# Batches of small matrix products in a recurrent scan: each batch queued behind one leader, and a 32-column product widened to 128

## The chip, the cores and the metric

The kernel runs on one core of a Trainium2 chip. The metric is the device time of one launch in microseconds (us); of the kernel before there are three timed runs with a median of 1272.58 us.

## The reference, cut to what matters

The model is a trunk of two residual layers over 512 tokens of width 1024. Layer 0 mixes tokens with a gated spatial MLP, layer 1 with an RWKV-7 recurrence; each is followed by a gated convolutional FFN, and a last RMSNorm ends it. The change lies in the recurrence, which has 16 heads of width 64:

```python
def step(state, inp):
    r_t, w_t, k_t, v_t, a_t, b_t = inp
    sa = jnp.einsum('bhvk,bhk->bhv', state, a_t)
    state = (state * w_t[:, :, None, :]
             + sa[..., None] * b_t[:, :, None, :]
             + v_t[..., None] * k_t[:, :, None, :])
    y_t = jnp.einsum('bhvk,bhk->bhv', state, r_t)
    return state, y_t
...
g = jax.nn.sigmoid(xg @ g1) @ g2          # g1: 1024 x 160, g2: 160 x 1024
...
return (y * g) @ w_o
```

The kernel doesn't step token by token. It cuts the 512 tokens into 8 chunks of 64 and does each chunk with small matrix products, so that only the 64 x 64 state of each head goes from chunk to chunk. The gate `g` needs a product with the 160 columns of `g1`, which the kernel does as 128 columns and 32 columns.

## The kernel before, in words

**The big products.** Nearly all arithmetic is 512 columns wide on TensorE. Each fp32 factor is split into a high and a low part, and a product becomes three matmuls, `mm3` (L313, its matmuls are L317, L318 and L319). Weights stream in from HBM ahead of their use.

**The scan.** `scan(g)` (L1168) runs for two groups g of 8 heads, one after the other, and in each over 8 chunks c. The 8 heads of a group are 4 pairs i of 2 heads `hd`; head `hd` = 0 lies on partitions 0 to 63, `hd` = 1 on 64 to 127. One chunk has five batches of 8 small products on TensorE, one for each `(i, hd)` in the list `ih`, and between them copies that hand the result on:

- L1194 (128 rows in, 64 columns out) makes `us` from the operand `vu`, which holds the state and the values of the chunk. L1196 copies `us` to `wt` on VectorE.
- L1198, of the same shape, makes the part of the output `e` that needs the same `vu` only.
- L1207 (64 x 64) multiplies `wt` by an inverse computed earlier. L1208 copies half 0 of the result into `vu` on VectorE, and L1209 copies half 1 on ScalarE.
- L1216 (128 x 64) makes the next state from `vu`. L1219 adds the decayed old state, half 0 and then half 1, on VectorE, and that is the operand `vu` of the next chunk's L1194.
- L1221 (64 x 64) adds the rest of `e`, which L1224 copies out on ScalarE.

So a chunk is a chain: L1194, L1196, L1207, L1208 and L1209, L1216, L1219, and again L1194. In two of these handovers the half `hd` = 1 is written after the half `hd` = 0.

**The filler.** While the chain waits for VectorE or ScalarE, TensorE does other work that is due anyway. `weave` advances the generator `fill`, which holds the value projections, the gates (`gates`, L1061) and the output projection (`project`), and queues each piece behind a mark in the chain; `side` is the inversion of the other group (L1030 and L1033, 32 x 32 products). `finish` (transposes, L1247) and `value` (L829, L844) come in between too. A scheduler then puts all instructions of an engine in one fixed order; with `tc.issue_after(x)` an instruction is kept behind x in the order of its engine, without a wait. In the scan before, the small products have no such order among them, and the scheduler may place each one by itself.

**The gate product.** `gates` multiplies 512 tokens by the 160 columns of `g1` in 8 steps over k. Each step has `mm3` with 128 columns and then `mm3` with 32 columns (128 rows in, 32 columns out); the 32 columns of each k lie next to each other in one weight tile, 256 columns in all. `gate_parts` (L300) loads it.

Of the kernel before, what the change touches and what calls it, by code (L numbers as in the profile page):

```python
# [12 lines left out]
F32 = mybir.dt.float32  # L13
F32R = mybir.dt.float32r
# [6 lines left out]
P = 128  # L21
D = 1024
KT = 8
# [121 lines left out]
class Emit:  # L145
# [154 lines left out]
    def gate_parts(self):  # L300

        t = [self.wp.tile([P, 1024], F32, tag="w32", bufs=2, name=self.uid("w32")) for _ in range(2)]
        for i in range(2):
            self.wq.dma_start(t[i], self.gd[:, i, 0:1024])
        return (1024, [tuple(x.bitcast(F32R) for x in t)]), (512, [self.pair(self.gd[:, :, 1024:], 256)])

    @staticmethod
    def wcols(w, c, n, rows=slice(None)):
# [423 lines left out]
    def rwkv_main(self, r, ctx, gain):  # L732
# [328 lines left out]
        def gates():  # L1061


            ws = ga["parts"]
            accs = [self.acc("mm")[0:n] for n in (P, 32)]
            for k in range(KT):
                x = gx[k]
                if k + 2 < KT:
                    gx.append(gate_mix(k + 2))
                for a, w, n in zip(accs, ws, (P, 32)):  # L1070
                    self.mm3(a, self.wcols(w, k * n, n), x, k == 0, k == KT - 1)
                next(tail[0], None)
                if k >= 3:
                    back(k - 3)
                yield
            for k in range(KT - 3, KT):
                back(k)
            for i, a in enumerate(accs):
                t = scratch("sq")[0:(P, 32)[i]]
                S.activation(t, a, AF.Tanh, scale=0.5)  # L1080
                V.tensor_scalar(t, t, 0.5, 0.5, ALU.mult, ALU.add)
                if i == 0:
                    S.copy(r.sg[0], t)
                    V.tensor_tensor(r.sg[1], t, r.sg[0].bitcast(F32), ALU.subtract)
                else:
                    self.stack(r.sg[2], t)
                yield
# [79 lines left out]

        def scan(g, late=iter(())):  # L1168

            ih = [(i, hd) for i in range(4) for hd in range(2)]  # L1170
            y = None

            for c in range(NCH):
                last = c == NCH - 1
# [10 lines left out]
                def ar(i, hd, n):  # L1185
                    o = C + P * hd + n * C
                    return st[i][:, o:o + C]

                def pt(i, hd):
                    o = RW * (1 - hd)  # L1190
                    return st[i][H[hd], o:o + C]

                for i, hd in ih:
                    nc.tensor.matmul(us[H[hd], 0, i, :], ar(i, hd, 0), vu[:, hd, i, :], start=True, stop=True)  # L1194
                wt = tile_([P, 4, C], "wt", 4)
                V.tensor_copy(wt, us[:, 0])  # L1196
                for i, hd in ih:
                    nc.tensor.matmul(e[H[hd], 0, i, :], ar(i, hd, 1), vu[:, hd, i, :],  # L1198
                                     start=i == 0, stop=False, skip_group_check=True)
                if not last:  # L1200
                    s0 = tile_([P, 4, C], "wt", 4)
                    for hd in range(2):
# [8 lines left out]
                if g == 1 and c == 0:  # L1211
                    self.step(late)
                yield
                if not last:
                    for i, hd in ih:
                        nc.tensor.matmul(us[H[hd], 0, i, :], bt[:, i, hd, :], vu[:, hd, i, :], start=True, stop=True)  # L1216
                    nvu = chunks[g, c + 1][2]
                    for hd in range(2):
                        V.tensor_tensor(nvu[H[hd], hd], us[H[hd], 0], s0[H[hd]], ALU.add)  # L1219
                for i, hd in ih:  # L1220
                    nc.tensor.matmul(e[H[hd], 0, i, :], pt(i, hd), vu[H[hd], hd, i, :],  # L1221
                                     start=False, stop=True, skip_group_check=True)
                for hd in range(2):
                    S.copy(y[H[c % 2], :, hd, :], e[H[hd], 0])  # L1224
                self.step(late)
# [169 lines left out]
```

## Time and profile before

| what | value |
|---|---|
| timed runs | 1272.14, 1272.58 and 1272.93 us; median 1272.58 us |
| the profiled execution's own time | 1274.33 us |
| its span, from the first to the last instruction | 1272.5 us |
| TensorE matmuls busy | 1254.8 us (99%) |
| TensorE weight loads busy | 1014.3 us (80%) |
| VectorE busy | 856.5 us (67%) |
| ScalarE busy | 629.6 us (49%) |
| GpSimd busy | 98.0 us (8%) |
| mean granted clock of TensorE | 0.994 |
| the stretch from 737 to 862 us, which holds the two scans: TensorE busy | 120.61 of 125.00 us |

In a timeline row the first number is the start in us, the second the length of the row, then the engine (PE is TensorE, DVE VectorE, ACT ScalarE, POOL GpSimd, PEld TensorE's weight loads), the line, the operation, out<-in by names, the size of the stationary operand (rows*columns), the shape, and how many records the row merges. The ends of matmuls are modelled and overlap the next matmul; what TensorE spends on something is read from one start to the next. A small fp32 product leaves two records, a batch of 8 leaves 16; a big one (`mm3`) leaves one record per matmul. Brackets at the end give the idle time ahead of a row and what ended it.

### The profile page before, as it was taken

The numbers are of one execution on the slowest core, as the hardware profiler recorded it, in microseconds if no ns is written. First come the engines' busy times: TensorE is split into PE (matmuls) and PEld (weight loads), VectorE is DVE, ScalarE is ACT, GpSimd is POOL, SyncE is SP. The second block draws the span as 40 slices with busy tenths as digits, with TensorE's granted clock in tenths as the row PEclk, the third lists the DMA queues.
The fourth block names the chain that finished last, engine by engine and source line by source line (L and its number), as shares of the span: only waits on it lengthen the run. The fifth ranks groups of instructions, "written<-read, shape, count | busy, mean of one in ns | idle before, by whom it ended". The sixth has DMA issues, their size and how long they took to land.

```text
span 1272.5 us, 19534 instructions
## 1 busy us (share of the span) xinstructions
PE 1254.8 (99%) x7591; PEld 1014.3 (80%) x7591; DVE 856.5 (67%) x1403; ACT 629.6 (49%) x1082; POOL 98.0 (8%) x119
## 2 busy tenths in 40 slices
PE   9999999999999999999999999999999999999997
PEld 6878888888888888887777776677888888888886
DVE  6466568888886444675789887665677777772233
ACT  5534446555555333475686647423544444443232
POOL 4100200000000000000000022222100000000002
PEclk9999999999999999999999999999999999999999
DMA  7332357887556775335878698763233332233332
GB/s 251 108 99 83 123 173 239 244 255 240 198 169 209 216 231 161 105 106 182 220 203 226 202 245 206 203 181 133 83 99 100 100 99 91 94 94 106 93 91 79
DMA packets 115452, 201.65 MB, mean 158 GB/s; under 512 B 21600, under 2 KB 53600, under 8 KB 115360
## 3 DMA queue, kind: packets, MB, share of 16 engines
q10 hardware_dynamic: 39104, 112.87, 29.4%
q1 hardware_dynamic: 76256, 87.54, 23.1%
q8 instruction: 59, 0.97, 0.3%
q14 instruction: 33, 0.27, 0.1%
HBM read 152.93 MB, written 47.45 MB: 157 GB/s over the span
## 4 chain that ended last, share of the span: by engine, by line
PE 90%; DVE 4%; issue 1%; DMA 0%; POOL 0%; ACT 0%; DVEq 0%; ACTq 0%; POOLq 0%
PE mm L317 10%; PE mm L319 9%; PE mm L318 9%; PE aux L317 6%; PE aux L319 6%; PE aux L318 6%; PE e L318 6%; PE e L317 6%; PE e L319 6%; PE us L319 5%; PE us L318 5%; PE us L317 5%; PE aux L935 1%; PE aux L949 1%; PE us L1194 1%; PE e L1221 1%
## 5 line engine op out<-in xcount | busy, mean ns | idle before, releaser
L236 ACT CAST w<-w 128x512 fp32r<-128x512 f32 x340 | 206.8, 611 | 364.6 <-PE aux L319 91.8
L237 DVE TENSOR_TENSOR w<-w,w 128x512 fp32r<-128x512 f32 x340 | 232.1, 685 | 185.2 <-ACT w L236 184.7
L317 PE MATMUL mm<-mxh,w 128*128 128x512 f32 (+1 forms) x416 | 170.5, 410 | 0.0
L318 PE MATMUL mm<-mxl,w 128*128 128x512 f32 (+1 forms) x416 | 164.6, 396 | 0.0
L319 PE MATMUL mm<-mxh,w 128*128 128x512 f32 (+1 forms) x416 | 164.3, 395 | 0.0
L344 POOL TENSOR_TENSOR ss<-ss,sq 128x512 f32<-128x512 f32 x30 | 40.6, 1353 | 771.1 <-issue 592.9
L317 PEld LDWEIGHTS mm<-mxh,w 128*128 128x128 f32 (+1 forms) x416 | 77.6, 187 | 20.0 <-issue 3.3
L319 PEld LDWEIGHTS mm<-mxh,w 128*128 128x128 f32 (+1 forms) x416 | 77.8, 187 | 17.4 <-issue 0.7
L318 PEld LDWEIGHTS mm<-mxl,w 128*128 128x128 f32 (+1 forms) x416 | 77.9, 187 | 16.1 <-issue 1.3
L542 ACT ACTIVATE cv<-z,par 128x512 f32<-128x512 f32 x88 | 71.7, 817 | 28.1 <-DVE z L540 23.1
L317 PE MATMUL aux<-mxh,w 128*128 128x512 f32 x216 | 84.5, 391 | 0.0
L319 PE MATMUL aux<-mxh,w 128*128 128x512 f32 x216 | 84.2, 390 | 0.3 <-DVE w L237 0.3
L317 PE MATMUL us<-mxh,w 128*128 128x512 f32 x216 | 84.5, 391 | 0.0
L318 PE MATMUL aux<-mxl,w 128*128 128x512 f32 x216 | 84.1, 389 | 0.0
L318 PE MATMUL us<-mxl,w 128*128 128x512 f32 x216 | 84.1, 389 | 0.0
L319 PE MATMUL us<-mxh,w 128*128 128x512 f32 x216 | 84.0, 389 | 0.0
L317 PE MATMUL e<-mxh,w 128*128 128x512 f32 x208 | 81.4, 391 | 0.1
L318 PE MATMUL e<-mxl,w 128*128 128x512 f32 x208 | 81.1, 390 | 0.1
L319 PE MATMUL e<-mxh,w 128*128 128x512 f32 x208 | 80.9, 389 | 0.0
L543 DVE SCALAR_TENSOR_TENSOR cv<-z,par,cv 128x512 f32<-128x512 f32 x88 | 66.1, 752 | 20.0 <-ACT cv L542 20.0
L544 DVE SCALAR_TENSOR_TENSOR cv<-z,par,cv 128x512 f32<-128x512 f32 x88 | 66.0, 752 | 2.9
L319 PEld LDWEIGHTS aux<-mxh,w 128*128 128x128 f32 x216 | 40.5, 187 | 9.2 <-DVE w L237 0.8
(1088 smaller groups left out, 2599.0 us busy)
## 6 DMA issues: line engine op xcount, KB each, us to landing
w<-in_wup ACTq DMA_DIRECT2D x88, 512.0 KB, 3.7
w<-in_wdn ACTq DMA_DIRECT2D x32, 512.0 KB, 3.6
st<-std SPq DMA_DIRECT2D x30, 320.0 KB, 6.1
w<-wkd ACTq DMA_DIRECT2D x16, 512.0 KB, 4.8
w<-wvd ACTq DMA_DIRECT2D x16, 512.0 KB, 5.6
w<-wod ACTq DMA_DIRECT2D x16, 512.0 KB, 4.3
w<-in_wdn ACTq DMA_DIRECT2D x16, 384.0 KB, 3.3
w<-in_wsu ACTq DMA_DIRECT2D x8, 512.0 KB, 3.8
```

The source lines that it names most:

```text
L236: nc.scalar.copy(hi[r, :n], src)
L237: (lo_eng or nc.vector).tensor_tensor(lo[r, :n], src, hi[r, :n].bitcast(F32), ALU.subtract)
L317: mm(acc, wh, xh, start=first, stop=False)
L318: mm(acc, wh, xl, start=False, stop=False)
L319: mm(acc, wl, xh, start=False, stop=last)
L344: nc.gpsimd.tensor_tensor(self.ss, self.ss, self.sq, ALU.add)
L542: nc.scalar.activation(c, z[:, 2:], AF.Identity, scale=cw(2, i), bias=self.p("conv_b", l * 44 + i))
L543: nc.vector.scalar_tensor_tensor(c, z[:, 1:T + 1], cw(1, i), c, ALU.mult, ALU.add)
L544: nc.vector.scalar_tensor_tensor(c, z[:, 0:T], cw(0, i), c, ALU.mult, ALU.add)
L935: nc.tensor.matmul(qs[hd][:, c - ch.start, :], bk[H[hd], c, C * hd:C * hd + P], ar[H[hd], c, :], start=True, stop=True)
L949: nc.tensor.matmul(qs[hd][:, c, :], bk[H[hd], c, C * hd:C * hd + P], dg[H[hd], c, :], start=True, stop=True)
L1194: nc.tensor.matmul(us[H[hd], 0, i, :], ar(i, hd, 0), vu[:, hd, i, :], start=True, stop=True)
```

## The change

Two things are changed. In `scan` a helper `batch` emits the 8 products of a batch; the list `ih` now has `hd` = 1 ahead of `hd` = 0 in each pair, and all products of a batch after the first are kept behind the first in TensorE's order (the leader). L1198's batch is kept behind the leader of L1194, and L1221's batch behind the leader of L1216. The batch of L1207 has the new order of `ih`, but no leader. In the gates the 32-column product now takes 128 columns: its own 32 and the 96 behind them in the tile; the accumulator has 128 rows, of which the last 96 are not read. The tile's columns 256 to 383, which no load fills, are set to zero on GpSimd.

```diff
@@ gate_parts
-        return (1024, [...]), (512, [self.pair(self.gd[:, :, 1024:], 256)])
+        w = self.pair(self.gd[:, :, 1024:], 256)
+        for x in w:
+            self.nc.gpsimd.memset(x[:, 256:384].bitcast(F32), 0.0)
+        return (1024, [...]), (512, [w])
@@ gates
-            accs = [self.acc("mm")[0:n] for n in (P, 32)]
+            accs = [self.acc("mm") for _ in range(2)]
...
-                    self.mm3(a, self.wcols(w, k * n, n), x, k == 0, k == KT - 1)
+                    self.mm3(a, self.wcols(w, k * n, P), x, k == 0, k == KT - 1)
...
-                S.activation(t, a, AF.Tanh, scale=0.5)
+                S.activation(t, a[0:(P, 32)[i]], AF.Tanh, scale=0.5)
@@ scan
-            ih = [(i, hd) for i in range(4) for hd in range(2)]
+            ih = [(i, hd) for i in range(4) for hd in (1, 0)]
+            def batch(one, lead=None):
+                for n, (i, hd) in enumerate(ih):
+                    with ExitStack() as behind:
+                        if lead is not None:
+                            behind.enter_context(tc.issue_after(lead))
+                        one(i, hd, n)
+                    if lead is None:
+                        lead = self.last(mybir.EngineType.PE)
+                return lead
...
-                for i, hd in ih:
-                    nc.tensor.matmul(us[H[hd], 0, i, :], ar(i, hd, 0), vu[:, hd, i, :], start=True, stop=True)
+                lead = batch(lambda i, hd, n: nc.tensor.matmul(us[H[hd], 0, i, :], ar(i, hd, 0), vu[:, hd, i, :],
+                                                               start=True, stop=True))
...
-                for i, hd in ih:
-                    nc.tensor.matmul(e[H[hd], 0, i, :], ar(i, hd, 1), ...)
+                batch(lambda i, hd, n: nc.tensor.matmul(e[H[hd], 0, i, :], ar(i, hd, 1), ...), lead)
...
+                lead = None
                 if not last:
-                    for i, hd in ih:
-                        nc.tensor.matmul(us[H[hd], 0, i, :], bt[:, i, hd, :], vu[:, hd, i, :], start=True, stop=True)
+                    lead = batch(lambda i, hd, n: nc.tensor.matmul(us[H[hd], 0, i, :], bt[:, i, hd, :], ...))
...
-                for i, hd in ih:
-                    nc.tensor.matmul(e[H[hd], 0, i, :], pt(i, hd), vu[H[hd], hd, i, :], ...)
+                batch(lambda i, hd, n: nc.tensor.matmul(e[H[hd], 0, i, :], pt(i, hd), ...), lead)
```

The order of the changed kernel prints its own line numbers. There L1207 and L1211 are the batches L1194 and L1198 of before, L1220 is L1207, L1229 is L1216, L1234 is L1221, L320 to L322 are L317 to L319, L832 is L829, L1107 is L1104 and L1260 is L1247.

TensorE's order in the first scan, from the end of a chunk into the next (in the trace of before this is 756.68 to 761.97 us). `us` and `e` are the accumulators of the batches, `mm` those of the filler. Before:

```order
L1221 MATMUL e_6839<-vu_6742,st_6738 64x64
L829 MATMUL mm_6982<-cst,v_6903 128x128 x3
L1216 MATMUL us_6838<-vu_6742,cbt_6741 64x64 x8
L1221 MATMUL e_6839<-vu_6742,st_6738 64x64 x7
L829 MATMUL mm_6982<-cst,v_6903 128x128
L317 MATMUL mm_6905<-mxh_5515,w_1094_6701 128x512
L1194 MATMUL us_6945<-vu_6742,st_6834 64x64
L1198 MATMUL e_6946<-vu_6742,st_6834 64x64
L318 MATMUL mm_6905<-mxl_5516,w_1094_6701 128x512
L1194 MATMUL us_6945<-vu_6742,st_6834 64x64 x7
L1198 MATMUL e_6946<-vu_6742,st_6834 64x64 x7
L1247 MATMUL aux_6968<-cst,y_6656 128x128 x4
```

The same place in the changed kernel:

```order
L832 MATMUL mm_6982<-cst,v_6903 128x128 x3
L1229 MATMUL us_6838<-vu_6742,cbt_6741 64x64 x8
L1234 MATMUL e_6839<-vu_6742,st_6738 64x64 x8
L832 MATMUL mm_6982<-cst,v_6903 128x128
L320 MATMUL mm_6905<-mxh_5515,w_1094_6701 128x512
L321 MATMUL mm_6905<-mxl_5516,w_1094_6701 128x512
L322 MATMUL mm_6905<-mxh_5515,w_1094_6701 128x512
L1207 MATMUL us_6945<-vu_6742,st_6834 64x64 x8
L1211 MATMUL e_6946<-vu_6742,st_6834 64x64 x8
L1260 MATMUL aux_6968<-cst,y_6656 128x128 x4
```

The single product that stood ahead of the filler is back in its batch, the pair ahead of L318 is back in its batches, and the filler that stood between the pair and the rest now stands ahead of both.

TensorE's order in the second scan, where the filler is the gate of one head group (accumulators `aux`; 814.93 to 820.06 us in the trace of before). Before:

```order
L1104 MATMUL aux_7775<-sg_6635,gw_6992 128x512
L317 MATMUL aux_7814<-sg_6633,gwh_6996 128x512
L318 MATMUL aux_7814<-sg_6634,gwh_6996 128x512
L1221 MATMUL e_7710<-vu_7533,st_7611 64x64
L319 MATMUL aux_7814<-sg_6633,gwl_6997 128x512
L1104 MATMUL aux_7814<-sg_6635,gw_6992 128x512
L1216 MATMUL us_7709<-vu_7533,cbt_7532 64x64 x8
L1221 MATMUL e_7710<-vu_7533,st_7611 64x64 x7
L1194 MATMUL us_7789<-vu_7705,st_7701 64x64
L1198 MATMUL e_7790<-vu_7705,st_7701 64x64
L1194 MATMUL us_7789<-vu_7705,st_7701 64x64 x7
L1198 MATMUL e_7790<-vu_7705,st_7701 64x64 x7
```

The same place in the changed kernel:

```order
L320 MATMUL aux_7816<-sg_6633,gwh_6996 128x512
L321 MATMUL aux_7816<-sg_6634,gwh_6996 128x512
L322 MATMUL aux_7816<-sg_6633,gwl_6997 128x512
L1229 MATMUL us_7711<-vu_7535,cbt_7534 64x64 x8
L1234 MATMUL e_7712<-vu_7535,st_7613 64x64 x8
L1107 MATMUL aux_7777<-sg_6635,gw_6992 128x512
L1107 MATMUL aux_7816<-sg_6635,gw_6992 128x512
L1207 MATMUL us_7791<-vu_7707,st_7703 64x64 x8
L1211 MATMUL e_7792<-vu_7707,st_7703 64x64 x8
```

Here the single product is back in its batch too, the pair had no filler behind it before, and the two products of L1104 moved from ahead of L1216 to between L1221 and the next chunk. Outside the two scans TensorE's order is the same in both kernels, SP's is the same everywhere, and VectorE and ScalarE have the same instructions with some of the filler's moved by a place or a few.

12 lines of the change are left out of this document (7 added, 5 removed).

## The prediction

> **What bounds the kernel now.** I read the page first, then busy time by stretches, then TensorE's timeline in the scan. The head of the page:
>
> ```profile
> span 1272.5 us, 19534 instructions
> PE 1254.8 (99%) x7591; PEld 1014.3 (80%) x7591; DVE 856.5 (67%) x1403; ACT 629.6 (49%) x1082; POOL 98.0 (8%) x119
> ```
>
> TensorE is busy for all but 18 us, so a gain has to be TensorE time. The stretch that holds both scans, and all behind it (columns: length, then busy time and records of PE, PEld, DVE, ACT, POOL, then granted clock, DMA share, GB/s):
>
> ```profile
> 737.00:862.00 125.00, 120.61 (x1754) 87.64 (x1753) 91.99 (x203) 59.63 (x120) 31.12 (x35) 1.00 0.80 205
> 865.00:1272.50 407.50, 397.57 (x1843) 331.70 (x1841) 245.51 (x369) 169.77 (x273) 23.86 (x24) 0.99 0.31 97
> ```
>
> The scan has few real waits, 4.4 us of 125. Behind it TensorE's order is unchanged and TensorE is nearly full, so what the scan saves stays saved at the end. But busy isn't useful here. TensorE's timeline around a single product of L1221 that stands alone in the filler, and a whole batch further on:
>
> ```profile
> 755.66 0.40 PE L319 MATMUL mm<-mxh,w 128*128 128x512 f32 x1
> 755.89 0.39 PE L317 MATMUL mm<-mxh,w 128*128 128x512 f32 x1
> ...
> 756.35 0.40 PE L319 MATMUL mm<-mxh,w 128*128 128x512 f32 x1
> 756.68 0.32 PE L1221 MATMUL e<-vu,st 64*64 64x64 f32 x2
> 756.94 0.94 PE L829 MATMUL mm<-cst,v 128*128 128x128 f32 x6
> ...
> 763.08 0.68 PE L1207 MATMUL us<-wt,ti 64*64 64x64 f32 x16
> 763.69 0.50 PE L317 MATMUL mm<-mxh,w 128*128 128x512 f32 x1
> 764.03 0.39 PE L318 MATMUL mm<-mxl,w 128*128 128x512 f32 x1
> ```
>
> Read the starts. In a row of big products one follows the other after 0.23 us (755.66, 755.89). The last one ahead of a small product keeps TensorE for 0.33 us (756.35 to 756.68), so 0.10 us goes into the change of size. The lone product takes 0.26 us, while a whole batch of eight takes 0.61 us (763.08 to 763.69). The first big product behind small ones takes 0.34 us (763.69 to 764.03), which is 0.11 us over its own pace. An excursion from the big size to a small one and back thus costs far more than the product in it, and the change takes excursions away.
>
> **What the change removes.** *Lone products of L1221.* One costs 0.10 + 0.26 + 0.11 = 0.47 us. I count nothing back for the batch that it was taken from (the next part shows why). The first and the last of the ten such pieces:
>
> ```profile
> 741.34 0.32 PE L1221 MATMUL e<-rb,mxh 64*64 64x64 f32 x2
> ...
> 836.96 0.33 PE L1221 MATMUL e<-vu,st 64*64 64x64 f32 x2
> ```
>
> Seven stand where TensorE is full: 7 x 0.47 = 3.3 us. Three (at 807.25, 815.82 and 821.99) stand in a stretch with waits, and there also a batch of L1216 is cut once by L844; these come below.
>
> *Pairs of L1194 and L1198.* The same with two products, and the batches that it is taken from, cut and whole:
>
> ```profile
> 768.38 0.40 PE L319 MATMUL mm<-mxh,w 128*128 128x512 f32 x1
> 768.71 0.33 PE L1194 MATMUL us<-vu,st 128*64 128x64 f32 x2
> ...
> 769.08 0.51 PE L317 MATMUL mm<-mxh,w 128*128 128x512 f32 x1
> ...
> 769.98 0.62 PE L1194 MATMUL us<-vu,st 128*64 128x64 f32 x13
> ...
> 771.06 0.49 PE L829 MATMUL mm<-cst,v 128*128 128x128 f32 x2
> ```
>
> ```profile
> 751.81 0.69 PE L1194 MATMUL us<-vu,st 128*64 128x64 f32 x16
> ...
> 752.89 0.50 PE L317 MATMUL mm<-mxh,w 128*128 128x512 f32 x1
> ```
>
> The change of size takes 0.10 us (768.38 to 768.71, less 0.23), the pair 0.37 us (to 769.08), the way back 0.11 us as above: 0.58 us. The batches without the pair take 1.08 us (769.98 to 771.06), whole ones 1.08 us (751.81 to 752.89), so nothing is given back. There are ten such pairs; the first and the last:
>
> ```profile
> 743.88 0.33 PE L1194 MATMUL us<-vu,st 128*64 128x64 f32 x2
> ...
> 855.85 0.33 PE L1194 MATMUL us<-vu,st 128*64 128x64 f32 x2
> ```
>
> Seven have filler between the pair and the rest: 7 x 0.58 = 4.1 us. In the other three (788.80, 811.44, 818.52) the rest follows at once, in the same size; they are worth nothing.
>
> **What is hidden by waits.** In the second scan, between 807 and 826 us, filler is short:
>
> ```profile
> 811.44 0.33 PE L1194 MATMUL us<-vu,st 128*64 128x64 f32 x2 [0.74 <-DVE vu L1219]
> 818.52 0.33 PE L1194 MATMUL us<-vu,st 128*64 128x64 f32 x2 [0.49 <-DVE vu L1219]
> 825.93 0.66 PE L1247 MATMUL aux<-cst,y 128*128 128x128 f32 x4 [0.80 <-DVE y L1243]
> ```
>
> TensorE that arrives earlier at these three waits only waits longer. What is removed ahead of them, three lone products at 0.26 to 0.47 us each and the cut of L1216 at a lone product's 0.26 us, is worth between 0 and 1.3 us. I take 0.3, near the lower end, since all of it lies ahead of a wait that exists.
>
> **The waits that the change adds.** No semaphore is added, but a batch now starts with the half that comes last. Behind a waiting leader stand its seven products, the sister batch, and all filler; VectorE's L1196 and ScalarE's L1224 wait for these. The handover from L1216 over L1219 to L1194, the one from L1207 over L1209 to L1216, and the length of a VectorE instruction that can be in the way:
>
> ```profile
> 749.53 0.69 PE L1216 MATMUL us<-vu,cbt 128*64 128x64 f32 x16
> 750.33 0.88 DVE L1219 TENSOR_TENSOR vu<-us,wt 64x256 f32<-64x256 f32 x2
> 751.70 1.10 DVE L237 TENSOR_TENSOR mxl<-sq,mxh 128x512 fp32r<-128x512 f32 x1
> ...
> 814.32 0.68 PE L1207 MATMUL us<-wt,ti 64*64 64x64 f32 x16
> 815.63 0.37 ACT L1209 COPY vu<-us 64x256 f32<-64x256 f32 x1 [2.28 <-DVE vu L1208]
> ```
>
> The second half of L1219 is done 1.68 us behind L1216's start (751.21). In the new order TensorE then has L1216 and L1221 (0.61 us each) and, where the order puts three big products in between, 0.34 + 0.23 + 0.33 = 0.90 us: it arrives after 2.1 us, and the wait is covered by 0.4 us. It shows only where VectorE is inside something long: up to 1.1 - 0.4 = 0.7 us. Of the 14 handovers I count two at 0.4 us, 0.8 us. From L1207 to L1216 the chain takes 1.68 us (814.32 to 816.00), and TensorE with three filler products arrives after 0.61 + 0.90 = 1.5 us; in the gate stretch that is some 0.2 us three times, 0.6 us. Together 1.4, say 1.5 us. The lower bound is 0 (all covered), the upper one a whole half of L1219 (0.88 / 2 = 0.44 us) uncovered in each of 14 chunks, 6.2 us. I stay near the lower bound because the rows show cover. The new order of `ih` costs L1208 one place in L1207's batch, a tenth of 0.61 us, inside the same cover; I count nothing.
>
> **The widened product.** The 24 matmuls with 32 columns stream 512 columns like the others. Their pace, their way back from a small size, and the weight loads:
>
> ```profile
> 794.52 0.40 PE L319 MATMUL mm<-mxh,w 128*128 128x512 f32 x1
> 794.75 0.40 PE L317 MATMUL mm<-mxh,w 128*32 128x512 f32 x1
> ...
> 775.27 0.43 PE L317 MATMUL mm<-mxh,w 128*32 128x512 f32 x1
> 775.54 0.39 PE L318 MATMUL mm<-mxl,w 128*32 128x512 f32 x1
> ```
>
> ```profile
> L319 PEld LDWEIGHTS mm<-mxh,w 128*128 128x128 f32 x8 | 1.5, 188 | 0.2
> L319 PEld LDWEIGHTS mm<-mxh,w 128*32 128x32 f32 x8 | 0.9, 109 | 0.8
> ```
>
> From 128 to 32 columns TensorE goes on at 0.23 us (794.52 to 794.75): that switch costs nothing, so taking it away gives nothing. The load gets 188 - 109 = 79 ns longer. In a row of products that hides under the 0.23 us; on the way back from a small batch it shows: 0.27 us with 32 columns (775.27 to 775.54) against 0.34 us with 128. Five of the 32-column products of before stand at such a place: 5 x 0.07 = 0.35 us lost. The two memsets on GpSimd stand between two pairs of L1203, and there GpSimd is idle for 6.21 us; two of a like size take 0.67 us:
>
> ```profile
> 750.89 1.37 POOL L1203 TENSOR_TENSOR wt<-vu,gc 64x256 f32<-64x256 f32 x2 [6.21 <-DVE vu L1219]
> 786.98 0.67 POOL L1161 MEMSET vu<- 64x256 f32 x2 [6.49 <-ACT ti L1038]
> ```
>
> That idle time hides them. Without it L1203, which L1219 needs one chunk later, would be 0.7 us late, once.
>
> Two rules of the Trainium skill bear on this. "TensorEngine Tiling (Array Packing)", Key Properties, says that a change of tiling mode, not just of tile, drains TensorE. For 64 columns the rows agree (0.10 us ahead, 0.11 us behind). For 32 columns they don't; by the rule six direct switches from 128 to 32 columns would go too, by an estimate at the 64-column rows' price 6 x 0.10 = 0.6 us more gain. "TensorE: Matmul & The Clock Gate", LDWEIGHTS (loading the stationary operand), speaks against the widening: the load's time goes with its columns over 1.2, by an estimate from that 80 ns more for each of 24, 1.9 us if none hides. The rows agree on the load (79 ns) but show it only where nothing covers it.
>
> **The sum.** 3.3 + 4.1 + 0.3 - 0.35 - 1.5 = 5.85, say 5.8 us. Against the profiled execution that is a span of 1272.5 - 5.8 = 1266.7 us and a time of 1274.33 - 5.8 = 1268.5 us. That execution took 1.8 us over the median of the timed runs, so the forecast is made on the median: 1272.6 - 5.8 = 1266.8 us.
>
> **The rivals.** *All of it counts.* No new wait, no loss in the widening and all 1.3 us of the hidden stretch: 3.3 + 4.1 + 1.3 = 8.7 us, 1263.9 us. For it speaks that VectorE mostly waits for TensorE at L1219, as the handovers show; against it the short filler in the gate stretch. Chance 0.10.
>
> *A wait takes the place of most of it.* If the second half of L1219 is uncovered in ten of 14 chunks, 10 x 0.44 = 4.4 us go: 3.3 + 4.1 + 0.3 - 0.35 - 4.4 = 2.95 us, and with VectorE in the way a little more often about 2 us, 1270.6 us. For it speaks that the filler of before ran in exactly those gaps; against it, that it still does, ahead of the batch. Chance 0.13.
>
> *The chain becomes the bound, and the kernel gets slower.* The early products did something: they ran inside the gap between the two halves. If neither the second half of L1219 (0.44 us) nor L1209 behind L1208 (0.37 us) is covered in any chunk, 14 x 0.81 = 11.3 us are added, and 11.3 - 7.35 = 3.9 us are lost, 1276.5 us. It decides from 7.35 / 14 = 0.53 us of new wait a chunk. Against it: the new order has three or more big products in nearly every gap. Chance 0.03.
>
> That the change doesn't do what it says is ruled out by the order: lone products and pairs are back in their batches.
>
> **How the numbers follow.** The forecast case has 0.74. Its own bounds are 3.3 + 4.1 + 1.3 - 0.35 = 8.35 us and 3.3 + 4.1 - 0.35 - 6.2 = 0.85 us; with the rivals I set the range from 1264.3 us (8.3 us gained) to 1270.4 us (2.2 us gained), which leaves out the ends of both. A measurement of this kernel tells 0.2% from no change, 2.5 us, so faster means under 1270.0 us. All of the first rival, nearly all of the forecast (0.72 of 0.74) and a little of the second (0.02) lie there: 0.84. Slower has the third rival's 0.03 and the rest, 0.13, is the same.
>
> **What would show it.** The timeline after should have no record of L1221's, L1194's or L1198's lines (new numbers 1234, 1207, 1211) alone between big products, and whole batches of 0.61 us; The scans should end some 6 us earlier, near 856 us instead of 862. Right for the wrong reason would be a gain behind 865 us. Wrong would be waits at the first product of a batch (by L1219 or L1209) that add up to over 5 us, or big products behind a batch that no longer pay 0.11 us. The rows with 128 columns in place of 32 should keep 0.23 us.

## The result, and the profile after

| what | before | after |
|---|---|---|
| median of 16 timed runs each | 1273.93 us | 1269.24 us |
| ratio, with its 95% interval | 1 | 0.9959 [0.9945, 0.9972] |
| profiled execution: own time, span | 1274.33, 1272.5 us | 1264.91, 1263.1 us |
| the two scans, first start of the first batch to last record of the last | 124.08 us (737.85 to 861.92) | 119.02 us (733.55 to 852.58) |

The ratio is 5.2 us of 1272.6, between 3.6 and 7.0 us; the forecast was 5.8 us. The spans of the two profiled executions differ by 9.4 us, which is more than the change did: TensorE's granted clock falls to about half for a few us in some executions and not in others, at places that differ from run to run. The windows just ahead of the scans, of before:

```profile
725.00:737.00 12.00, 12.00 (x144) 9.68 (x144) 9.53 (x23) 6.35 (x15) 1.25 (x2) 0.72 0.66 177
...
728.00:732.00 4.00, 4.00 (x43) 3.32 (x43) 3.56 (x14) 2.21 (x6) 0.00 (x0) 0.50 0.45 137
```

TensorE is busy through all 12 us, at a clock of 0.72 over them and 0.50 within, so 12 x 0.28 = 3.4 us are lost there. The window from 15 to 30 us has a clock of 0.89 before and 1.00 after, another 1.7 us. After has a clock of 1.00 from 600 us to the scans. So the length of the two scans, in which the clock is 1.00 in both kernels, is the better measure between single profiles, and I use it below as "the scans". Their windows, of before and then of after (length, then busy time of PE, PEld, DVE, ACT, POOL, then clock, DMA share, GB/s):

```profile
737.80:862.10 124.30, 119.91 (x1752) 87.28 (x1751) 91.32 (x201) 58.86 (x119) 31.12 (x35) 1.00 0.79 204
```

```profile
733.50:852.80 119.30, 111.56 (x1752) 84.63 (x1751) 92.01 (x203) 59.25 (x119) 31.14 (x37) 1.00 0.84 215
```

The same 1752 matmul records take 8.35 us less of TensorE, and TensorE's idle time grows from 4.4 to 7.7 us. So some three fifths of what was saved arrives. Behind the scans nothing is gained or lost: 410.4 us from there to the end before and 410.3 us after, and in windows of 410.0 us TensorE is busy for 400.57 us before and 400.14 us after.

A single length of the scans isn't good to 0.1 us, though. Six kernels of the experiments below change nothing in the scans, whose TensorE order is that of the changed kernel; there, less what a drop of the clock inside took, they lasted 116.7 to 118.7 us, against 119.0 us here. Part of that spread is the "issue" stops that are explained below.

The timeline of TensorE where the prediction showed a lone product of L1221 (now L1234) and the pair of L1194 and L1198 (now L1207 and L1211), in the changed kernel:

```profile
752.12 0.83 PE L832 MATMUL mm<-cst,v 128*128 128x128 f32 x6
752.88 0.69 PE L1229 MATMUL us<-vu,cbt 128*64 128x64 f32 x16
753.49 0.68 PE L1234 MATMUL e<-vu,st 64*64 64x64 f32 x16
754.10 0.49 PE L832 MATMUL mm<-cst,v 128*128 128x128 f32 x2
754.35 0.48 PE L320 MATMUL mm<-mxh,w 128*128 128x512 f32 x1
754.66 0.39 PE L321 MATMUL mm<-mxl,w 128*128 128x512 f32 x1
754.89 0.40 PE L322 MATMUL mm<-mxh,w 128*128 128x512 f32 x1
755.22 0.69 PE L1207 MATMUL us<-vu,st 128*64 128x64 f32 x16
```

Each batch has its 16 records in one row, one batch takes 0.61 us (752.88 to 753.49), and there is no lone product. Over both scans one batch is still cut: six products of L1229 start at 768.07, three big ones follow, and the last two start at 769.74. Before, a batch of L1216 was cut in the same way by L844 (807.51 to 809.17). Of the big products only those next to a batch pay: 0.33 us ahead of it (754.89 to 755.22), 0.31 us behind small ones (754.35 to 754.66).

What TensorE waited for in the scans (total us, times, longest), before and then after; "issue" is a stop that no event in the profile explains:

```profile
PE aux L1033 <- issue: 1.3, 1, 1.3
PE us L1194 <- DVE vu L1219: 1.2, 2, 0.7
PE aux L1247 <- DVE y L1243: 0.8, 1, 0.8
PE aux L1030 <- issue: 0.5, 1, 0.5
PE aux L318 <- DVE sg L1084: 0.2, 1, 0.2
```

```profile
PE us L1220 <- DVE wt L1210: 2.2, 3, 0.8
PE aux L1260 <- DVE y L1256: 1.3, 3, 0.8
PE aux L1033 <- issue: 1.1, 1, 1.1
PE aux L1036 <- issue: 0.9, 1, 0.9
PE us L1207 <- PE e L1234: 0.5, 1, 0.5
PE us L1207 <- PE aux L1260: 0.4, 1, 0.4
PE us L1229 <- ACT vu L1222: 0.3, 1, 0.3
```

Behind these stand three of 0.15 to 0.20 us. Without "issue" the single waits add up to 2.2 us before and 5.2 us after.

The wait that the prediction feared most, by L1219 (now L1233) at a chunk's first batch, seems to be gone, but it stands under other names. The view puts three waits of L1207, 1.1 us together, down to TensorE's own products (L1234, L1260 and L1107). The longest of them, with VectorE's L1233 just ahead of it:

```profile
816.02 0.88 DVE L1233 TENSOR_TENSOR vu<-us,wt 64x256 f32<-64x256 f32 x2
...
817.00 0.69 PE L1207 MATMUL us<-vu,st 128*64 128x64 f32 x16 [0.48 <-PE e L1234]
```

L1234 had ended at 816.51, the second half of L1233 at 816.90, and the batch starts 0.10 us behind that. The other two start 0.10 us behind the second half of L1233 too (804.27 and 811.11). At the place of the longest one, the kernel with the batches alone (below; L1204 and L1230 are its L1207 and L1233) has the wait under the right name:

```profile
PE us L1204 <- DVE vu L1230: 0.5, 1, 0.5
```

So this handover still costs 1.1 us, in three chunks, against 1.2 us in two before. What is new stands elsewhere: the largest row is the handover over L1210, the copy of `us` to `wt` (L1196 before), which the prediction didn't price. VectorE's timeline shows why, at the longest of these waits (0.80 us, until TensorE starts L1220 at 813.49):

```profile
811.04 1.29 DVE L1109 TENSOR_TENSOR rt<-rt,aux 128x512 f32<-128x512 f32 x2
812.41 0.69 DVE L1114 TENSOR_TENSOR mxl<-rt,mxh 128x512 fp32r<-128x512 f32 x1
813.02 0.42 DVE L1210 COPY wt<-us 128x256 f32<-128x256 f32 x1
```

L1210 needs only L1207's batch, which TensorE started at 811.11. But it stands behind three long instructions of the gates in VectorE's fixed order, and on TensorE a single big product stands between L1211 and L1220.

### The profile page after: what moved, and what is told of

Read it like the earlier page. It is cut to its first block, busy times and chain, and to the rows that moved or that the text cites. A ratio compares the mean times of both kernels' runs of the same rounds, so it can differ in the third digit from the quotient of the medians.

```text
span 1263.1 us, 19531 instructions
## 1 busy us (share of the span) xinstructions
PE 1241.9 (98%) x7591; PEld 1007.9 (80%) x7591; DVE 856.1 (68%) x1403; ACT 629.7 (50%) x1082; POOL 98.0 (8%) x121
## 4 chain that ended last, share of the span: by engine, by line
PE 86%; DVE 6%; DMA 1%; issue 1%; ACT 1%; POOL 0%; SPq 0%; DVEq 0%; ACTq 0%; POOLq 0%
PE mm L320 9%; PE mm L322 9%; PE mm L321 9%; PE aux L320 6%; PE aux L322 6%; PE aux L321 6%; PE e L321 6%; PE e L320 6%; PE e L322 6%; PE us L321 5%; PE us L322 5%; PE us L320 5%; PE aux L938 1%; DVE tt L1015 1%; DVE pr L1014 1%; PE aux L952 1%
## 5 line engine op out<-in xcount | busy, mean ns | idle before, releaser
L320 PE MATMUL mm<-mxh,w 128*128 128x512 f32 x416 | 169.7, 408 | 0.2 <-ACT vt L837 0.2
L321 PE MATMUL mm<-mxl,w 128*128 128x512 f32 x416 | 163.8, 394 | 0.0
L322 PE MATMUL mm<-mxh,w 128*128 128x512 f32 x416 | 163.7, 394 | 0.0
L320 PEld LDWEIGHTS mm<-mxh,w 128*128 128x128 f32 x416 | 78.1, 188 | 20.1 <-issue 3.3
L322 PEld LDWEIGHTS mm<-mxh,w 128*128 128x128 f32 x416 | 78.2, 188 | 16.7 <-issue 0.7
L321 PEld LDWEIGHTS mm<-mxl,w 128*128 128x128 f32 x416 | 78.2, 188 | 15.5 <-issue 1.3
L322 PE MATMUL aux<-mxh,w 128*128 128x512 f32 x216 | 84.2, 390 | 0.3 <-DVE w L237 0.3
L320 PE MATMUL aux<-mxh,w 128*128 128x512 f32 x216 | 84.5, 391 | 0.0
L320 PE MATMUL us<-mxh,w 128*128 128x512 f32 x216 | 84.5, 391 | 0.0
L321 PE MATMUL aux<-mxl,w 128*128 128x512 f32 x216 | 84.1, 389 | 0.0
L321 PE MATMUL us<-mxl,w 128*128 128x512 f32 x216 | 84.1, 389 | 0.0
L322 PE MATMUL us<-mxh,w 128*128 128x512 f32 x216 | 84.0, 389 | 0.0
L320 PE MATMUL e<-mxh,w 128*128 128x512 f32 x208 | 81.4, 391 | 0.1
L321 PE MATMUL e<-mxl,w 128*128 128x512 f32 x208 | 81.1, 390 | 0.1
L322 PE MATMUL e<-mxh,w 128*128 128x512 f32 x208 | 80.9, 389 | 0.0
L546 DVE SCALAR_TENSOR_TENSOR cv<-z,par,cv 128x512 f32<-128x512 f32 x88 | 66.1, 752 | 19.9 <-ACT cv L545 19.9
L322 PEld LDWEIGHTS aux<-mxh,w 128*128 128x128 f32 x216 | 40.5, 188 | 9.2 <-DVE w L237 0.8
```

Source lines behind the costliest of these rows:

```text
L320: mm(acc, wh, xh, start=first, stop=False)
L321: mm(acc, wh, xl, start=False, stop=False)
L322: mm(acc, wl, xh, start=False, stop=last)
L546: nc.vector.scalar_tensor_tensor(c, z[:, 1:T + 1], cw(1, i), c, ALU.mult, ALU.add)
```

## The experiments

Theory: an excursion to a small size and back costs some 0.47 us, the change takes excursions away, and what it gains is that less the new waits. The rivals were a drain at each switch to 32 columns, an excursion that is cheap by itself, and that the order of the halves or the leaders alone do the work.

**The two parts apart.** The gate's product left at 32 columns, the batches as changed (against the changed kernel; the memsets go too):

```diff
...
-            accs = [self.acc("mm") for _ in range(2)]
+            accs = [self.acc("mm")[0:n] for n in (P, 32)]
...
-                    self.mm3(a, self.wcols(w, k * n, P), x, k == 0, k == KT - 1)
+                    self.mm3(a, self.wcols(w, k * n, n), x, k == 0, k == KT - 1)
```

> The batches as in the changed kernel, the gate product left at 32 columns. The scan stretch is the time from the first start of the first batch (us from vu) to the first record of the last output batch's end (e from vu): 124.1 us before, 119.0 us in the changed kernel. Its order has as many excursions from the big size to a small one as the changed kernel (102 against 116 before) and eight direct switches from 128 to 32 columns. Theory 1 (each excursion costs 0.5 us, a switch between 128 and 32 columns costs nothing, the longer weight load shows only behind a small batch): 118.8 us, that is the changed kernel less 0.2 us; ratio 0.9957. Theory 2 (a switch to 32 columns drains like one to 64): 0.8 to 1.7 us longer than the changed kernel, 119.8 to 120.7 us; ratio 0.997.

Measured: ratio 0.9955 [0.9943, 0.9967]. The scans took 121.51 us, but with a drop of the clock inside (0.66 from 787 to 792 us, 5 x 0.34 = 1.7 us) and with 3.2 us of "issue" stops against 2.0 us. Less the 1.7 and the 1.2 us that these differ by it is 118.6 us, near the theory's 118.8, but a number that needs two corrections of that size doesn't tell 0.5 us. The ratio shows that the batches alone bring all that can be measured.

The widening alone, the scan's small products as before (against the kernel before; the memsets come too):

```diff
...
-            accs = [self.acc("mm")[0:n] for n in (P, 32)]
+            accs = [self.acc("mm") for _ in range(2)]
...
-                    self.mm3(a, self.wcols(w, k * n, n), x, k == 0, k == KT - 1)
+                    self.mm3(a, self.wcols(w, k * n, P), x, k == 0, k == KT - 1)
```

> The widened gate product alone, the scan as before. The order has as many excursions as before (116) and six direct switches from 128 to 32 columns fewer. Theory 1: scan stretch 124.1 + 0.35 = 124.4 us, ratio 1.000. Theory 2 (a switch to 32 columns drains): 0.6 to 1.2 us shorter, 122.9 to 123.5 us, ratio 0.9993.

Measured: ratio 0.999 [0.9975, 1.0004], the scans 124.31 us against 124.08 before. The window of the scans in this kernel:

```profile
732.70:857.30 124.60, 120.24 (x1752) 89.15 (x1751) 92.95 (x204) 59.07 (x119) 32.21 (x37) 1.00 0.79 206
```

TensorE is busy 0.3 us longer, as the prediction had it (0.35), and nothing is gained. The 124.31 us hold 0.9 us of "issue" stops where before has 1.9 us, and a wait of 0.9 us that before hasn't; without the stops and that wait they are 122.5 us against 122.2 us. So the shortening of 0.6 to 1.2 us that a drain at 32 columns would have brought isn't there. This profile holds one more thing, that first wait in the scan:

```profile
735.25 0.68 PE L1210 MATMUL us<-wt,ti 64*64 64x64 f32 x16 [0.89 <-DVE wt L1199]
```

It is the first chunk's handover over the copy to `wt`, and this kernel has the batches of before. The same wait of 0.77 to 0.89 us stands in every kernel whose clock didn't drop just ahead of the scans, the changed one among them (0.77), and is missing in the three profiles whose clock did: before, a run with extra products of 32 columns (0.72 from 736 to 748 us) and the one with a higher rate of filler (0.72 from 724 to 736 us). So 0.8 us of the waits after aren't the change's: a TensorE at half clock would let VectorE catch up. That cause is inferred from which runs have it; no run set the clock.

**Halves and leaders apart.** The leaders kept, the halves in the old order:

```diff
-            ih = [(i, hd) for i in range(4) for hd in (1, 0)]
+            ih = [(i, hd) for i in range(4) for hd in (0, 1)]
```

> The changed kernel with the halves in the old order: the leader of a batch is a product whose operand comes first. The order has 107 excursions (102 in the changed kernel, 116 before) and 248 switches of size (236, 274). Theory 1 (excursions set the time): five excursions at 0.5 us dearer than the changed kernel, 121.5 us in the scan stretch, ratio 0.9978. Rival (what counts is that a batch can start with the half that is ready, and the new waits of the changed kernel go): as short as the changed kernel or shorter, 117 to 119 us.

Measured: ratio 0.9962 [0.9949, 0.9975], the scans 123.03 us with 1.7 us lost to the clock inside (0.66 from 789 to 794 us), so 121.3 us. TensorE's waits in it, the two largest rows:

```profile
PE us L1207 <- DVE vu L1233: 2.1, 3, 0.9
PE aux L1036 <- issue: 1.6, 1, 1.6
```

The expectation of 121.5 us for excursions that set the time held. But waits aren't what makes this kernel longer: without "issue" they add up to 3.8 us, against 5.2 us in the changed kernel, for the waits by L1210 in the gates go, as the rival had it, while those by L1233 grow from 1.1 to 2.1 us. TensorE has more work:

```profile
734.40:857.70 123.30, 117.32 (x1752) 88.79 (x1751) 92.02 (x204) 59.18 (x119) 31.79 (x37) 0.99 0.81 208
```

Less the 1.7 us of the clock it is busy for 115.6 us, against 111.56 us: 4 us more, where five excursions at 0.5 us were expected to cost 2.5, and the shorter waits make up for the rest. In ten chunks the first product of L1207, with that of L1211, stands ahead of its batch again, as the pairs did before; the lone products of L1234 (L1221 before) are gone. A leader keeps its batch behind itself, but doesn't keep other work from coming in between. The ratio doesn't tell this kernel from the changed one; the scans do, by some 2 us: without clock and "issue" 119.5 us, against 116.7 to 118.2 us in the changed kernel and the kernels of the same order.

The halves in the new order, the leaders taken away:

```diff
-                        if lead is not None:
+                        if False:
                             behind.enter_context(tc.issue_after(lead))
```

> The changed kernel without the order edges behind the leader: only the halves are turned round. The order of all engines is word for word that of the changed kernel, so whatever the theory this is the changed kernel once more: scan stretch 119.0 us, ratio 0.996. It shows how well the scan stretch and the ratio repeat, and that the edges do nothing here.

Measured: ratio 0.9963 [0.9949, 0.9976], the scans 118.94 us against 119.02 of the changed kernel. Every engine's order is word for word that of the changed kernel. So the leaders do nothing here: with the half that comes last asked for first, the scheduler places no product of L1207, L1211 or L1234 ahead of its batch. And two profiles of the same order, with "issue" stops of a like size (2.0 and 1.8 us), agree in this stretch within 0.1 us.

**The price of an excursion, by itself.** Six kernels add one product ahead of each of the 88 groups of big products in the FFNs' up-projections, far from the scan, where TensorE is full. The group's first product overwrites it. The first of them, and what the others put in its place:

```diff
                     a = self.acc()
+                    nc.tensor.matmul(a[0:64, 0:64], self.c("ident", 64, slice(0, 64)),
+                                     self.c("ident", 64, slice(0, 64)), start=True, stop=True)
                     self.dense(a, w, x)
```

```diff
+nc.tensor.matmul(a[:, 0:64], self.c("ident", P), self.c("ident", 64), start=True, stop=True)
+nc.tensor.matmul(a[0:32], self.wcols(w, 0, 32)[0], x[0][0], start=True, stop=True)
+nc.tensor.matmul(a[0:64], self.wcols(w, 0, 64)[0], x[0][0], start=True, stop=True)
+nc.tensor.matmul(a[0:64, 0:64], self.c("ident", 64), self.c("ident", 64), start=True, stop=True)
+nc.tensor.matmul(a[0:64], self.wcols(w, 0, 64, slice(0, 64))[0], x[0][0][0:64], start=True, stop=True)
```

> The changed kernel with one small product of 64 rows, 64 columns and 64 elements (fp32, two records, as the lone products of the scan before) ahead of each of the 88 groups of big products of the FFNs' up-projections; the group's first product overwrites it, so the output stays the reference's. TensorE is full there and nothing is removed, so this prices an excursion by itself. Theory (0.10 us ahead, 0.26 us in the product, 0.11 us behind, 0.47 us in all): 88 x 0.47 = 41 us longer than the changed kernel. Rival (the lone products of before filled time that was idle anyway, an excursion itself is cheap, at most the 0.08 us that one of eight in a batch takes): 7 us.

> The control to the product of 64 x 64: the same 88 places and the same 64 elements in fp32 (two records), but 128 rows and 128 columns, the size of its neighbours, so no change of size. Theory (the size's change is what costs): clearly under the 41 us of the small product, two passes at some 0.1 us each, 88 x 0.2 = 18 us, and the big product behind it starts without the 0.11 us. Rival (what costs is the change of type from the big products' fp32r to fp32, or the load of a lone product): as much as with 64 x 64, 36 to 41 us.

> A product of 128 rows and 32 columns with 512 elements in the type of the big products ahead of each of the 88 groups, between products of 128 x 128: the direct change of 128 to 32 columns and back, 88 times each way. Theory (that change costs nothing, the product takes the pace of its neighbours): 88 x 0.23 = 20 us longer than the changed kernel. By the rule of the Trainium skill, page TensorEngine Tiling (Array Packing), section Key Properties, that a change of the tiling mode drains TensorE, the price of the rows of 64 columns would come on top, 88 x 0.21 = 18 us: 38 us.

> As the run with 32 columns, with 64 columns: 128 rows, 64 columns, 512 elements, same type as the big products, 88 places. Theory (64 columns are a change of size, as in the scan's batches of 128 x 64: 0.10 us ahead and 0.11 us behind): 88 x (0.23 + 0.21) = 39 us longer than the changed kernel. Rival (fewer columns in the big products' own type are no change at all, it is the 64 rows or fp32 that cost): 20 us, as with 32 columns.

> The changed kernel with one fp32 product of 128 rows, 64 columns and 64 elements (two records) ahead of each of the 88 groups of big products of the FFNs' up-projections, overwritten by the group's first product. It separates columns from rows and type: at the same places an fp32 product of 64 x 64 was reached 0.09 us late and took 0.255 us, one of 128 x 128 was reached at the pace and took 0.14 us, and one of 128 x 64 in the big products' type was reached at the pace. Theory A (in fp32 fewer columns are a change of size, as the pairs of the scan before show): 0.09 us ahead, about 0.25 us in the product, 0.45 us in all, 88 x 0.45 = 40 us longer than the changed kernel. Theory B (only fewer rows are a change of size): reached at the pace, 0.14 us in the product, 0.22 us in all, 20 us.

> As the run with 128 rows, 64 columns and 512 elements in the big products' own type (fp32r), with 64 rows: 88 products of 64 x 64 with 512 elements. Theory B (fewer rows are the change of size, whatever the type): 0.09 us ahead and something in the product on top of its 0.23 us, 0.4 us in all, 88 x 0.4 = 35 us longer than the changed kernel. Theory A (the change of size shows in fp32 alone): 88 x 0.23 = 20 us.

Two of their timelines, the product of 64 x 64 and then its control of 128 x 128 (L533 is the added line):

```profile
279.46 0.39 PE L322 MATMUL e<-mxh,w 128*128 128x512 f32 x1
279.78 0.33 PE L533 MATMUL us<-cst 64*64 64x64 f32 x2
280.03 0.50 PE L320 MATMUL us<-mxh,w 128*128 128x512 f32 x1
280.37 0.39 PE L321 MATMUL us<-mxl,w 128*128 128x512 f32 x1
```

```profile
281.07 0.39 PE L322 MATMUL us<-mxh,w 128*128 128x512 f32 x1
281.30 0.33 PE L533 MATMUL mm<-cst 128*128 128x64 f32 x2
281.44 0.48 PE L320 MATMUL mm<-mxh,w 128*128 128x512 f32 x1
281.75 0.40 PE L321 MATMUL mm<-mxl,w 128*128 128x512 f32 x1
```

Read from start to start, as in the prediction: 0.32, 0.25 and 0.34 us around the small product, 0.23, 0.14 and 0.31 us around the control. Three more, with 64 columns in the big products' own type, the same columns in fp32, and 64 rows in the big products' type:

```profile
280.23 0.40 PE L533 MATMUL mm<-mxh,w 128*64 128x512 f32 x1
280.46 0.39 PE L320 MATMUL mm<-mxh,w 128*128 128x512 f32 x1
```

```profile
284.55 0.39 PE L322 MATMUL us<-mxh,w 128*128 128x512 f32 x1
284.87 0.33 PE L533 MATMUL mm<-cst 128*64 128x64 f32 x2
285.12 0.50 PE L320 MATMUL mm<-mxh,w 128*128 128x512 f32 x1
```

```profile
283.10 0.39 PE L322 MATMUL e<-mxh,w 128*128 128x512 f32 x1
283.42 0.45 PE L533 MATMUL us<-mxh,w 64*64 64x512 f32 x1
283.79 0.50 PE L320 MATMUL us<-mxh,w 128*128 128x512 f32 x1
```

The medians over the 87 or 88 places. The price is what the three intervals add to a row of big products at 0.227 us; the last column is the difference between the kernel's timed ratio and the changed kernel's 0.9959, times 1273.9 us:

| added product | last big one to it | it to the next | next to the one after | price | 88 times | timed |
|---|---|---|---|---|---|---|
| 64 x 64, fp32, 64 elements | 0.318 | 0.255 | 0.335 | 0.45 us | 40.0 us | 34.9 us |
| 128 x 128, fp32, 64 elements | 0.228 | 0.138 | 0.314 | 0.23 us | 19.9 us | 18.2 us |
| 128 x 32, fp32r, 512 elements | 0.226 | 0.236 | 0.228 | 0.24 us | 20.8 us | 18.9 us |
| 128 x 64, fp32r, 512 elements | 0.226 | 0.236 | 0.228 | 0.24 us | 20.8 us | 16.8 us |
| 128 x 64, fp32, 64 elements | 0.318 | 0.258 | 0.338 | 0.46 us | 40.5 us | 41.4 us |
| 64 x 64, fp32r, 512 elements | 0.318 | 0.375 | 0.333 | 0.57 us | 50.3 us | 50.7 us |

The intervals of the timed column reach 3 to 6 us to either side, and no price falls outside. The expectation for 64 x 64 held (41 us), the rival of a cheap excursion (7 us) falls. The control is half as dear, so the type alone isn't the cause. A drain at 32 columns falls (38 us expected by it). My own expectation for 128 x 64 in fp32r falls too: 39 us, and it costs no more than a big product, as its rival had it. Neither theory A nor B of the last two holds alone, and 64 x 64 in fp32r is dearer than either had it (35 us). In fp32r a change of size is paid with 64 rows and not with 64 columns alone. In fp32 it is paid with 64 columns already, and 64 rows add nothing to it (0.45 against 0.46 us). Why the type decides for the columns stays open; the fp32 product also has fewer elements and two passes, and no run separates these.

**A try at a better version.** If the waits by L1210 come from short filler in the gates, more filler there should help. Two gate pieces in a step of the filler, and a higher rate of filler in the second scan:

```diff
-                yield
+                if i % 2 == 1:
+                    yield
```

```diff
-RATES = (..., (0.72, 2), (2, 2), (1.2, 6, 2.2))
+RATES = (..., (0.8, 2), (2, 2), (1.2, 6, 2.2))
```

> The changed kernel with two of the gate's four pieces in each step of the filler instead of one, so that five to eight big products stand between a chunk's first batches and the batch that needs the copy of L1210 where there were one to three. Theory (the new waits of the changed kernel are at the handover over L1210 in the gate stretch, because the filler there is short and the copy stands behind the gate's own work in VectorE's order): its 2.2 us of waits by L1210 fall under 1 us and TensorE's idle time in the scans from 7.5 to some 6 us; 1 to 1.5 us faster than the changed kernel, a ratio to the kernel before of some 0.995. Rival (VectorE is the bound there, so that more gate work earlier makes the copy later still): the waits by L1210 stay at 2 us or grow, and no gain.

> The changed kernel with the second scan's rate of filler at 0.8 steps a mark instead of 0.72, which brings a fourth gate piece and the output projection earlier, so that three big products instead of one stand ahead of the second handover over L1210 and seven instead of three behind it. Theory: the wait of 0.8 us by L1210 at the second gate chunk and the 0.5 us at the next chunk's first batch go, the one of 0.6 us ahead of it stays; 1 us faster than the changed kernel, ratio some 0.995. Rival (filler that is brought forward is missing at the scan's end): the waits come back behind 842 us, no gain.

Measured: 0.9965 [0.9952, 0.9979] and 0.9955 [0.9941, 0.9968]. Neither can be told from the changed kernel, and the 1 us that was expected isn't there: their scans hold 12 matmul records more than the changed kernel's, so the kernels are compared from the scans' start to the end of the kernel, less the clock's drops inside the scans, and that is 529.2 and 529.6 us, against 529.6 us in the changed kernel. TensorE's waits of some size in the first of them (its lines from L1107 on stand one further down), and then in the second:

```profile
PE us L1221 <- DVE wt L1211: 1.6, 2, 0.8
PE aux L1033 <- issue: 1.3, 1, 1.3
PE us L1230 <- ACT vu L1223: 0.9, 2, 0.6
PE aux L320 <- DVE rt L1110: 0.8, 1, 0.8
```

```profile
PE us L1220 <- DVE wt L1210: 1.5, 2, 0.8
PE aux L1036 <- issue: 1.2, 1, 1.2
PE us L1229 <- ACT vu L1222: 1.0, 3, 0.4
```

In the first both of the copy's waits in the gates (0.63 and 0.80 us) are gone, but 0.61 us by ScalarE's copy L1223 and 0.83 us by VectorE's L1110 stand there instead, and TensorE waits 0.85 us for the copy at a later chunk (827.92 us): the gates' own chain through VectorE is next. The clock dropped in this profile from 814 to 819 us (0.66), ahead of that last wait, so its size is not a clean one. In the second the first of the two stays at 0.64 us, and the other goes and comes back as 0.83 us at a later chunk (823.48 us). Its rival had waits coming back too, but behind 842 us; the rest of its fall is the first chunk's wait, which the clock spared it. So the waits in the gates seem to have several causes of nearly the same lateness, and taking one away shows the next. A copy of `wt` that VectorE does ahead of the gates' work was not tried.

## Why the prediction was right, step by step

*The work saved.* The terms of the sum without the waits, with all of the hidden stretch counted, were 3.3 + 4.1 + 1.3 - 0.35 = 8.35 us; TensorE's busy time in the scans fell by 119.91 - 111.56 = 8.35 us. That the two agree to the last digit is luck: the pieces of the hidden stretch, as the prediction lists them, add up to 1.04 to 1.67 us and not to 1.3. The size of a lone product's price is settled by the added products, 0.45 to 0.46 us each against 0.47. That nothing is given back for its batch holds too: where a big product follows, the batches of L1221 with 14 records took 0.60 us and those with 16 took 0.61 us. The pairs' 0.58 us was read from rows only; no added product prices it.

*How that price is made up.* Here the prediction read one thing wrongly. It put the 0.11 us behind a small product down to the change of size. The control changes no size and pays 0.314 - 0.227 = 0.09 us there as well. The control takes 0.14 us, and a weight load for 128 columns 188 ns in the rows of before, so the load of the next big product can't hide under it whole. Its trace fits: the load for L321 starts 0.08 us behind L320's start (281.52 us), where in a row of big products a load starts with the product ahead (280.85 us). No run separates the load from the change of type. The Trainium skill's page "TensorE: Matmul & The Clock Gate", Step-by-step: what each phase is for, has the next weights load while the current matmul runs, so a short matmul would cover little of it. What the size itself costs is 0.454 - 0.226 = 0.23 us: 0.09 us ahead, 0.12 us longer in the product, 0.02 us behind. The sum was right because it was taken from rows as a whole.

*The rule on tiling.* "TensorEngine Tiling (Array Packing)" in the Trainium skill, Key Properties, lets a change of tiling mode drain TensorE. The runs show extra time, as a drain would bring it, with 64 x 64 in either type and with 128 x 64 in fp32, and none with 128 x 32 or 128 x 64 in fp32r (0.226 us ahead, 0.228 us behind). The 0.6 us that the rule would have added for the widening wasn't there.

*The new waits.* This is the term that was mis-sized: 1.5 us forecast, 5.2 - 2.2 = 3.0 us found. 0.8 us of it is the first chunk's, which the kernel with the old batches has too; 2.2 us are the change's. The two handovers that were priced came out under their price: by L1233 (0.8 us forecast) 1.1 us stand in three chunks, but 1.2 us stood there before, so nothing is added; by L1222 (0.6 us forecast) there is 0.3 us. The rest is at places that weren't looked at: 0.63 + 0.80 us by L1210 in the gates, where the prediction had noted that the filler is short and moved, but had asked only for L1219 and L1209; 0.45 us more by the norm's L1256; and 0.2 us ahead of a filler product at 768.85.

*The balance.* TensorE saves 8.35 us and stands idle for 3.35 us more: 3.0 us of these waits, 0.1 us of "issue", the rest in stops too short for the view. That leaves 5.0 us, and the scans are 124.08 - 119.02 = 5.06 us shorter; with the first chunk's wait in both kernels it would be some 5.8 us, by an estimate from that wait. Two terms of the sum were off and made up for each other in part: without the new waits, 7.35 us were counted as saved and TensorE saved 8.35 us; 1.5 us were counted as new waits and 3.0 us were there. The forecast case held with less gain than its 5.8 us. "A wait takes the place of most of it" named the right kind of loss, at the wrong handover and too large. The chain didn't become the bound: by L1233 and L1222, which were feared in all 14 chunks, TensorE waits for 1.4 us in all, in four places.

*What the change does.* The prediction reasoned from leaders behind which a batch stands. They aren't what makes the batches whole: the order of the halves is, and without the leaders the order is the same. With the leaders alone the lone products of L1221 go back, but ten pairs of L1194 and L1198 stay ahead of their batches.

*The widening.* -0.35 us forecast; alone it made TensorE 0.3 us busier and the scans, without "issue" stops and the first chunk's wait, 0.3 us longer.

## What to carry to other kernels

Price an excursion of TensorE to another size from start to start, over the product and both its neighbours, and add a control of the same length without the change of size before naming a cause. When early pieces of a batch are given up, follow every handover of the chain through the other engines' fixed order, the first as well as the last: TensorE arrives earlier at all of them, and here the one that was late next was the copy that stands behind the filler's own work. When a view names a producer that had ended long before the wait did, look for another one that ended just ahead of it. And when an order falls apart, look for what makes a scheduler see one piece ready first; here, putting the operand that comes last at the head mended it without any constraint.

## What the runs showed of the hardware that was not expected

- Fewer columns in fp32r are no change of size: 128 x 32 and 128 x 64 take 0.236 us among 128 x 128 at 0.227 us. In fp32 128 x 64 pays 0.23 us more than 128 x 128, and 64 x 64 in fp32r pays 0.57 - 0.24 = 0.33 us more than 128 x 64.
- The granted clock drops to half for stretches that cost 1.7 or 3.4 us, in some executions and at places that move. That is more than the parts of this change differ by. By the Trainium skill's page "TensorE: Matmul & The Clock Gate", What's actually happening, the clock is set by how busy TensorE was in a free-running window of about 3.4 us; a loss of 1.7 us is one such window at half clock, by an estimate from that page (3.4 x 0.5), and the moving places fit. That only an idle window drops it doesn't fit the rows of before: from 725 to 737 us TensorE is never idle. Ahead of that drop stand small products of 64 elements (L949, from 723.85 us); whether these count as idle wasn't tried.
- TensorE's "issue" stops in the scans, most of them ahead of the 32 x 32 products of the inverse (L1033 and L1036), took 0 to 2.0 us in eight profiles of the same order, and 3.2 us in the kernel with the gate at 32 columns. In the kernels with the control products and with 128 x 64 in fp32r they were absent, and the scans took 116.7 and 117.2 us against 119.02 with the same order. No run shows what they are.
